# A macaron encoder block: three plain gate chunks at the start of the first feed-forward block, four block pairs instead of five, and another order at both openings

## The chip, the cores and the metric

The kernel runs on one core of one Trainium2 chip. The metric is device microseconds of one execution, as the median of several runs. The engines are called as in the profile: PE (TensorE, matrix products), DVE (VectorE), ACT (ScalarE), POOL (GpSimd) and SP (SyncE, which issues all loads).

## What is computed

One layer for 256 tokens of width 2048, all in float32. The change touches the two feed-forward blocks, the first and the last big stage:

```python
def _swiglu(x, wg, wu, wd):
    return (jax.nn.silu(x @ wg) * (x @ wu)) @ wd
h = h + 0.5 * _swiglu(_rmsnorm(h, ffn1_norm[i]), ffn1_wg[i], ffn1_wu[i], ffn1_wd[i])
a = _rmsnorm(h, mix_norm[i])
z = a @ w_in[i]                   # q, k, v of 8 heads; three parts of a gated short convolution
...
h = h + mixed @ w_out[i]
h = h + 0.5 * _swiglu(_rmsnorm(h, ffn2_norm[i]), ffn2_wg[i], ffn2_wu[i], ffn2_wd[i])
...                               # a gated per-layer embedding
return _rmsnorm(h, final_norm)
```

`wg` and `wu` are 2048 x 5632, `wd` is 5632 x 2048. The 5632 hidden columns are eleven chunks of 512.

## The kernel before

**Precision and tiles.** Each float32 operand is split into a high part (ACT, a copy to the PE's rounded format) and a low part (DVE, the difference). A product is three matmuls (`mm3`, lines 114 to 116): high x high, high x low, low x high. Weights come in tiles of 128 x 1024 (512 KB): SP loads `raw`, ACT writes `whi`, DVE writes `wlo`. There are 6 buffers each of `raw`, `whi` and `wlo`, so a tile can be prepared at most 6 tiles ahead of the one that PE works on.

**Items.** `unit_items` makes a unit of one chunk: 8 items for a gate or up chunk (`g0`, `u0`, `u1`, ...), 2 items for a column of `d0` (the down product of chunk 0), 4 for later down columns. An item has a preparation (load and split a tile) and a run (12 matmuls of 512 columns: 4 triples). `drive` lines the items up: it emits preparations until 6 tiles are held and then the run of the oldest item, so on ACT and DVE the work of an item stands behind the preparation of items up to 6 tiles later. After each run `pump()` emits one entry of `queue`, the side work: transposes of a finished chunk, factors, SiLU of a pair. Then, if it was the unit's last item, `done` emits the unit's eviction. The order so written holds on each engine.

**Banks.** A unit writes two PSUM tiles. With `wide` false they are always those with the tag `mm`, of which there are two: the next unit's first matmul waits until the unit before is evicted. With `wide` true the units go to `pa` and `mm` by turns.

**Pairs.** The gate product is done for chunk 0 by itself and for chunks 1 to 10 as five pairs by Winograd's form of Strassen's scheme: 7 half-size products in place of 8. A pair (`Pair`, names `ffn1s0` to `ffn1s4`) is 12 items: 8 of two tiles and 4 triples each, then 4 of three tiles and 6 triples, 56 triples in all where two plain gate chunks are 64; DVE has additions on the raw tiles besides. It uses combinations of the four quarters of the activations: `factors` makes them, one half chunk (c, p) a call, by four small DVE subtractions (`ffn1sv`), an ACT copy (`ffn1sh`) and a DVE difference (`ffn1sl`). `at` and `base` are the places in the stream of plain items ahead of which a pair's items stand. At a pair's end `whole` combines (6 DVE operations), then `queue` gets SiLU (ACT, 4 operations), `after` (products with the up chunk, lines 486 and 490) and `turn` (transposes).

**The norm.** The scale 1/rms is applied at the evictions. In the first block `load_x` loads `h` during `u0` and sums its squares on ACT; at the end of `u0`, `silu0` makes the scale (DVE, then POOL), applies SiLU to `g0` (`ffn1sg`) and `gated` (line 448) multiplies it with `u0`; then the transposes `ffn1gT` stand behind the next item's run. In the second block the scale is made by a queue entry.

**The opening of a block** is `g0`, `u0`, `u1`, `u2`, `d0` with pair 0 between their items.

Of the kernel before, what the change touches and what calls it, by code (L numbers as in the profile page):

```python
# [944 lines left out]
```

## Time and profile before

| what | value |
|---|---|
| median of 3 runs | 1963.72 us (1963.34 to 1965.5) |
| the profiled execution | 1965.0 us |
| its span, first to last instruction | 1962.9 us |
| mean granted TensorE clock | 0.989 of full speed |
| PE busy | 1910.3 us, 97% of the span |
| DVE busy, ACT busy | 1473.9 us, 1056.6 us |
| bytes read from HBM | 433.41 MB, 222 GB/s over the span |

The profiled execution is one of its own; 2.1 us of its time lie outside its span. A busy PE counts the modelled end of each matmul, so neighbouring matmuls overlap in the rows: the pace is read from start to start. "Idle before" a row is the time in which the engine did nothing, with what released it.

### The profile page before, as it was taken

The numbers are of one execution on the slowest core, as the hardware profiler recorded it, in microseconds if no ns is written. First come the engines' busy times: TensorE is split into PE (matmuls) and PEld (weight loads), VectorE is DVE, ScalarE is ACT, GpSimd is POOL, SyncE is SP. The second block draws the span as 40 slices with busy tenths as digits, with TensorE's granted clock in tenths as the row PEclk, the third lists the DMA queues.
The fourth block names the chain that finished last, engine by engine and source line by source line (L and its number), as shares of the span: only waits on it lengthen the run. The fifth ranks groups of instructions, "written<-read, shape, count | busy, mean of one in ns | idle before, by whom it ended". The sixth has DMA issues, their size and how long they took to land.

```text
span 1962.9 us, 23890 instructions
## 1 busy us (share of the span) xinstructions
PE 1910.3 (97%) x8649; PEld 1578.6 (80%) x8649; DVE 1473.9 (75%) x1712; ACT 1056.6 (54%) x1345; POOL 35.7 (2%) x36
## 2 busy tenths in 40 slices
PE   8898999999999999999999989989999999999998
PEld 6686888888888888888888868868888888888887
DVE  6877978879788765656656668778797887987664
ACT  7554555555555555555445555545555555555653
POOL 0000000000000000100000000000000000000010
PEclk9998999999999999999999999989999999999999
DMA  8575776777767765555555547747777667777652
GB/s 293 196 259 186 265 265 225 264 251 245 266 223 240 270 201 183 192 172 165 177 190 177 187 163 230 273 163 260 253 244 271 222 239 268 240 269 238 204 182 99
DMA packets 127206, 437.09 MB, mean 223 GB/s; under 512 B 13808, under 2 KB 14320, under 8 KB 126832
## 3 DMA queue, kind: packets, MB, share of 16 engines
q1 hardware_dynamic: 127088, 435.57, 65.7%
q8 instruction: 68, 1.11, 0.2%
q14 instruction: 50, 0.41, 0.1%
HBM read 433.41 MB, written 2.10 MB: 222 GB/s over the span
## 4 chain that ended last, share of the span: by engine, by line
PE 92%; DVE 3%; ACT 3%; issue 1%; DMA 1%; POOL 0%; ACTq 0%; SPq 0%; POOLq 0%; DVEq 0%
PE ffn2u L114 4%; PE ffn2u L116 4%; PE ffn2u L115 4%; PE ffn1d L114 4%; PE ffn2d L114 4%; PE ffn1d L116 4%; PE ffn1d L115 4%; PE ffn2d L116 4%; PE ffn2d L115 4%; PE ffn1u L114 4%; PE ffn1u L116 4%; PE ffn1u L115 4%; PE o L114 1%; PE o L116 1%; PE o L115 1%; PE pg L116 1%
## 5 line engine op out<-in xcount | busy, mean ns | idle before, releaser
L45 ACT ACTIVATE whi_ffn1s<-raw_ffn1s 128x1024 fp32r<-128x1024 f32 x120 | 126.2, 1061 | 169.6 <-DVE raw_ffn1s L347 38.0
L45 ACT ACTIVATE whi_ffn2s<-raw_ffn2s 128x1024 fp32r<-128x1024 f32 x120 | 126.0, 1061 | 165.3 <-DVE raw_ffn2s L347 39.7
L110 DVE TENSOR_TENSOR wlo_ffn2s<-raw_ffn2s,whi_ffn2s 128x1024 fp32r<-128x1024 f32 x120 | 144.6, 1221 | 14.0 <-ACT whi_ffn2s L45 9.7
L110 DVE TENSOR_TENSOR wlo_ffn1s<-raw_ffn1s,whi_ffn1s 128x1024 fp32r<-128x1024 f32 x120 | 144.7, 1221 | 11.1 <-ACT whi_ffn1s L45 6.5
L114 PE MATMUL ffn2u<-whi_ffn2u,aTh 128*128 128x512 f32 x352 | 138.5, 393 | 7.4 <-ACT ffn2sg L45 7.4
L114 PE MATMUL ffn1u<-whi_ffn1u,aTh 128*128 128x512 f32 x352 | 139.3, 396 | 5.7 <-DVE ffn1sg L448 3.4
L115 PE MATMUL ffn1u<-wlo_ffn1u,aTh 128*128 128x512 f32 x352 | 138.7, 394 | 4.0 <-DVE wlo_ffn1u L110 4.0
L110 DVE TENSOR_TENSOR wlo_ffn2u<-raw_ffn2u,whi_ffn2u 128x1024 fp32r<-128x1024 f32 x88 | 106.0, 1221 | 43.6 <-ACT whi_ffn2u L45 42.4
L116 PE MATMUL ffn1u<-whi_ffn1u,aTl 128*128 128x512 f32 x352 | 138.1, 392 | 0.0
L115 PE MATMUL ffn2u<-wlo_ffn2u,aTh 128*128 128x512 f32 x352 | 137.7, 391 | 0.0
L116 PE MATMUL ffn2u<-whi_ffn2u,aTl 128*128 128x512 f32 x352 | 137.7, 391 | 0.0
L110 DVE TENSOR_TENSOR wlo_ffn1u<-raw_ffn1u,whi_ffn1u 128x1024 fp32r<-128x1024 f32 x88 | 105.7, 1221 | 38.2 <-ACT whi_ffn1u L45 37.2
L45 ACT ACTIVATE whi_ffn2u<-raw_ffn2u 128x1024 fp32r<-128x1024 f32 x88 | 91.1, 1055 | 63.9 <-PE ffn2u L116 45.0
L110 DVE TENSOR_TENSOR wlo_ffn2d<-raw_ffn2d,whi_ffn2d 128x1024 fp32r<-128x1024 f32 x88 | 104.9, 1219 | 17.4 <-ACT whi_ffn2d L45 17.2
L45 ACT ACTIVATE whi_ffn1u<-raw_ffn1u 128x1024 fp32r<-128x1024 f32 x88 | 90.7, 1054 | 50.5 <-PE ffn1u L116 40.8
L110 DVE TENSOR_TENSOR wlo_ffn1d<-raw_ffn1d,whi_ffn1d 128x1024 fp32r<-128x1024 f32 x88 | 104.7, 1220 | 12.4 <-ACT whi_ffn1d L45 12.0
L45 ACT ACTIVATE whi_ffn2d<-raw_ffn2d 128x1024 fp32r<-128x1024 f32 x88 | 89.3, 1048 | 16.3 <-PE ffn2d L116 8.0
L45 ACT ACTIVATE whi_ffn1d<-raw_ffn1d 128x1024 fp32r<-128x1024 f32 x88 | 89.2, 1048 | 11.3 <-PE ffn1d L116 5.1
L114 PEld LDWEIGHTS ffn1u<-whi_ffn1u,aTh 128*128 128x128 f32 x352 | 66.6, 189 | 21.9 <-ACT whi_ffn1u L45 4.4
L114 PEld LDWEIGHTS ffn2u<-whi_ffn2u,aTh 128*128 128x128 f32 x352 | 66.6, 189 | 21.4 <-ACT ffn2sg L45 7.8
L115 PEld LDWEIGHTS ffn1u<-wlo_ffn1u,aTh 128*128 128x128 f32 x352 | 66.8, 190 | 19.6 <-DVE wlo_ffn1u L110 6.0
L116 PEld LDWEIGHTS ffn1u<-whi_ffn1u,aTl 128*128 128x128 f32 x352 | 66.7, 189 | 13.8
(809 smaller groups left out, 5108.9 us busy)
## 6 DMA issues: line engine op xcount, KB each, us to landing
raw_ffn1s<-in_ws SPq DMA_DIRECT2D x120, 512.0 KB, 5.5
raw_ffn2s<-in_ws SPq DMA_DIRECT2D x120, 512.0 KB, 5.4
raw_ffn1u<-in_wu SPq DMA_DIRECT2D x88, 512.0 KB, 5.1
raw_ffn1d<-in_wd SPq DMA_DIRECT2D x88, 512.0 KB, 4.9
raw_ffn2u<-in_wu SPq DMA_DIRECT2D x88, 512.0 KB, 5.1
raw_ffn2d<-in_wd SPq DMA_DIRECT2D x88, 512.0 KB, 4.8
raw_o<-in_wout SPq DMA_DIRECT2D x32, 512.0 KB, 4.5
raw_pg<-in_wpg SPq DMA_DIRECT2D x24, 512.0 KB, 4.6
```

The source lines that it names most:

```text
L45: nc.scalar.activation(out=out, in_=in_, func=func, **kw)
L110: tt(out=lo[:, sl], in0=raw[:, sl], in1=f(hi[:, sl]), op=ALU.subtract)
L114: nc.tensor.matmul(ps, lhsT=xh, rhs=wh, start=first, stop=False)
L115: nc.tensor.matmul(ps, lhsT=xh, rhs=wl, start=False, stop=False)
L116: nc.tensor.matmul(ps, lhsT=xl, rhs=wh, start=False, stop=last)
```

## The change

The first block no longer uses a pair for chunks 1 and 2: `first_opening` runs `g0`, `u0`, `g1`, `u1`, `d0`, `g2`, `u2` as plain units with `wide` true, and four pairs follow for chunks 3 to 10 (`quads(w, 1536)`). The calls of `factors` are spread: one for every second item of `u0` and `g1`, where before there was one for every item of `u0`. In `unit_items` the eviction of a finished unit is emitted ahead of the side work, where it stood behind it. In the second block the entry that makes the norm's scale stands ahead of the four factor entries, pair 0 stands at earlier places (`at` ends at 32, not 36), and the second product of `after` is a queue entry of its own. `WK` goes from 10 to 11 work buffers.

```diff
-    WK = 10
+    WK = 11
@@ unit_items, run
-            pump()
+            due = min(1, len(queue))
             if g == ng - 1 and s == 1:
                 done(st["ps"])
+            pump(due)
@@ Pair.whole
-            queue.extend([lambda: (silu(0), silu(1)), self.after, lambda: None, self.turn])
+            queue.extend([lambda: (silu(0), silu(1)), self.after]
+                         + [lambda: None] * self.gap + [self.turn])
@@ swiglu, pair
-            pr = Pair(nm, ws, i, gate)
+            pr = Pair(nm, ws, i - 1 if first else i, gate)
...
+            def after_b():
+                for t in range(2):
+                    tt(out=pr.c[2 * t + 1], in0=pr.ub[t], in1=pr.c[2 * t + 1], op=ALU.mult)
+                queue.append(turned([pr.c[1], pr.c[3]], 2, pr.sets))
...
                 if i == 0:
-                    for t in range(2):
-                        tt(out=pr.c[2 * t + 1], in0=pr.ub[t], in1=pr.c[2 * t + 1], op=ALU.mult)
-                    queue.append(turned([pr.c[1], pr.c[3]], 2, pr.sets))
+                    queue.append(after_b)
@@ swiglu
+        def both_plain(fc, g, sets, hooks):
+            if fc > 0:
+                def done(ps):
+                    for t in range(2):
+                        act(g[t], ps[t], AF.Silu, scale=gate["rstd"][:, t:t + 1])
+                yield from unit_items(wg, fc, f"{nm}g{fc}", aT, done, wide=True, late=hooks[0])
+
+            def done_up(pu):
+                if fc == 0:
+                    silu0()
+                gated(pu, g)
+                queue.append(turned(g, fc, sets))
+            yield from unit_items(wu, fc, f"{nm}u{fc}", aT, done_up, wide=True, late=hooks[1])
+
+        def first_opening(pr):
+            sets0 = []
+
+            def hook(o):
+                def late(g, s):
+                    if o == 0 and s == 0:
+                        load_x(g)
+                    if s == 0:
+                        factors(nm, o + g // 2, g % 2)
+                return late
+            yield from both_plain(0, g0, sets0, (None, hook(0)))
+            g1 = [wk(f"{nm}sg1_{t}") for t in range(2)]
+            yield from both_plain(1, g1, pr.sets, (hook(2), None))
+            yield from down(0, 1, sets0, False, True)
+            g2 = [wk(f"{nm}sg2_{t}") for t in range(2)]
+            yield from both_plain(2, g2, pr.sets, (None, None))
@@ swiglu, everything
                 yield from gate0(early)
-                at = [8, 10, 12, 14, 16, 18, 20, 21, 23, 24, 26, 28]
-                base = 32
+                at = []
+                base = 48
             else:
+                queue.append(lambda: gate.update(rstd=rstd_of(nm)))
                 for c in (2, 3):
                     for p in range(2):
                         queue.append(partial(factors, nm, c, p))
-                queue.append(lambda: gate.update(rstd=rstd_of(nm)))
-                at = [8, 11, 14, 16, 19, 22, 24, 26, 29, 32, 34, 36]
+                at = [8, 10, 13, 16, 18, 20, 22, 24, 26, 28, 30, 32]
                 base = 40
```

**Place A, the first block's first gated chunk.** On DVE, up to the gated product of `g0` (`ffn1sg0`), which the transposes wait for; before:

```order
L347 TENSOR_TENSOR raw_ffn1s0_0_0_524<-raw_ffn1s0_0_0_524,raw_ffn1s0_0_1_526 128x512
L348 TENSOR_TENSOR raw_ffn1s0_0_1_526<-raw_ffn1s0_0_0_524,raw_ffn1s0_0_1_526 128x512
L349 TENSOR_TENSOR raw_ffn1s0_0_1_526<-raw_ffn1s0_0_1_526,raw_ffn1s0_0_0_524 128x512
L110 TENSOR_TENSOR wlo_ffn1s0_0_0_532<-raw_ffn1s0_0_0_524,whi_ffn1s0_0_0_531 128x1024
L110 TENSOR_TENSOR wlo_ffn1s0_0_1_536<-raw_ffn1s0_0_1_526,whi_ffn1s0_0_1_535 128x1024
L110 TENSOR_TENSOR wlo_ffn1u1_0_0_554<-raw_ffn1u1_0_0_551,whi_ffn1u1_0_0_553 128x1024
L110 TENSOR_TENSOR wlo_ffn1u1_0_1_572<-raw_ffn1u1_0_1_569,whi_ffn1u1_0_1_571 128x1024
L225 TENSOR_REDUCE sm_ffn1_None_599<-ss_ffn1_0_339 128x1
L225 TENSOR_REDUCE sm_ffn1_None_599<-ss_ffn1_1_401 128x1
L228 TENSOR_SCALAR sm2_ffn1_None_602<-sm_ffn1_None_599 128x2
L448 SCALAR_TENSOR_TENSOR ffn1sg0_0_104<-ffn1u0_0_446,rstd_ffn1_None_604,ffn1sg0_0_104 128x512
L448 SCALAR_TENSOR_TENSOR ffn1sg0_1_105<-ffn1u0_1_447,rstd_ffn1_None_604,ffn1sg0_1_105 128x512
```

and in the changed kernel:

```order
L110 TENSOR_TENSOR wlo_ffn1g1_2_0_573<-raw_ffn1g1_2_0_570,whi_ffn1g1_2_0_572 128x1024
L318 TENSOR_TENSOR ffn1sv3_0_578<-a3_0_228 128x128
L319 TENSOR_TENSOR ffn1sv3_0_578<-a3_0_228 128x128
L320 TENSOR_TENSOR ffn1sv3_0_578<-a3_0_228,ffn1sv3_0_578 128x128
L321 TENSOR_TENSOR ffn1sv3_0_578<-a3_0_228,ffn1sv3_0_578 128x128
L323 TENSOR_TENSOR ffn1sl3_577<-ffn1sv3_0_578,ffn1sh3_576 128x4x128
L226 TENSOR_REDUCE sm_ffn1_None_597<-ss_ffn1_0_332 128x1
L226 TENSOR_REDUCE sm_ffn1_None_597<-ss_ffn1_1_385 128x1
L229 TENSOR_SCALAR sm2_ffn1_None_600<-sm_ffn1_None_597 128x2
L450 SCALAR_TENSOR_TENSOR ffn1sg0_0_104<-ffn1u0_0_423,rstd_ffn1_None_602,ffn1sg0_0_104 128x512
L450 SCALAR_TENSOR_TENSOR ffn1sg0_1_105<-ffn1u0_1_424,rstd_ffn1_None_602,ffn1sg0_1_105 128x512
L110 TENSOR_TENSOR wlo_ffn1g1_2_1_613<-raw_ffn1g1_2_1_610,whi_ffn1g1_2_1_612 128x1024
```

The two tiles of pair 0 and two of `u1` ahead of the norm have gone; five tiles of `g1` and three factor steps (of c = 2 and 3) stand ahead of it. On PE the transposes stood behind `u0`, one pair item and one item of `u1`; now they stand behind `u0` and one item of `g1`.

**Place C, the opening of the second block.** On ACT, from the last tile of `g0` (`ffn2g0_3_1`) to its SiLU (`ffn2sg0`); before:

```order
L45 ACTIVATE ffn2sh2_9291<-ffn2sv2_0_9293 128x4x128
L45 ACTIVATE ffn2sh2_9291<-ffn2sv2_1_9312 128x4x128
L45 ACTIVATE whi_ffn2s0_0_0_9326<-raw_ffn2s0_0_0_9319 128x1024
L45 ACTIVATE whi_ffn2s0_0_1_9330<-raw_ffn2s0_0_1_9321 128x1024
L45 ACTIVATE ffn2sh3_9346<-ffn2sv3_0_9348 128x4x128
L45 ACTIVATE whi_ffn2u0_0_0_9357<-raw_ffn2u0_0_0_9355 128x1024
L45 ACTIVATE ffn2sh3_9346<-ffn2sv3_1_9373 128x4x128
L45 ACTIVATE whi_ffn2u0_0_1_9382<-raw_ffn2u0_0_1_9380 128x1024
L45 ACTIVATE whi_ffn2u0_1_0_9407<-raw_ffn2u0_1_0_9405 128x1024
L45 ACT_TABLE_LOAD
L45 ACTIVATE ffn2sg0_0_9179<-ffn2g0_0_9217,rstd_ffn2_None_9403 128x512
```

and in the changed kernel:

```order
L45 ACTIVATE ffn2sh2_9207<-ffn2sv2_0_9209 128x4x128
L45 ACTIVATE whi_ffn2s0_0_0_9223<-raw_ffn2s0_0_0_9216 128x1024
L45 ACTIVATE whi_ffn2s0_0_1_9227<-raw_ffn2s0_0_1_9218 128x1024
L45 ACTIVATE ffn2sh2_9207<-ffn2sv2_1_9243 128x4x128
L45 ACTIVATE whi_ffn2u0_0_0_9252<-raw_ffn2u0_0_0_9250 128x1024
L45 ACTIVATE ffn2sh3_9268<-ffn2sv3_0_9270 128x4x128
L45 ACTIVATE whi_ffn2u0_0_1_9279<-raw_ffn2u0_0_1_9277 128x1024
L45 ACTIVATE ffn2sh3_9268<-ffn2sv3_1_9295 128x4x128
L45 ACT_TABLE_LOAD
L45 ACTIVATE ffn2sg0_0_9076<-ffn2g0_0_9114,rstd_ffn2_None_9193 128x512
```

The factor copies (`ffn2sh`) stand apart from one another, the third tile of `u0` has gone behind the SiLU, and the last factor copy still stands ahead of it.

**Place D, the end of the second block's pair 0.** On DVE, from the last tile of the `d0` columns 0 to 3 (`ffn2d0_3_0_1`) to the eviction of column 2 into `h`; before:

```order
L110 TENSOR_TENSOR wlo_ffn2d0_3_0_1_10348<-raw_ffn2d0_3_0_1_10345,whi_ffn2d0_3_0_1_10347 128x1024
L347 TENSOR_TENSOR raw_ffn2s1_0_0_10351<-raw_ffn2s1_0_0_10351,raw_ffn2s1_0_1_10353 128x512
L348 TENSOR_TENSOR raw_ffn2s1_0_1_10353<-raw_ffn2s1_0_0_10351,raw_ffn2s1_0_1_10353 128x512
L349 TENSOR_TENSOR raw_ffn2s1_0_1_10353<-raw_ffn2s1_0_1_10353,raw_ffn2s1_0_0_10351 128x512
L110 TENSOR_TENSOR wlo_ffn2s1_0_0_10359<-raw_ffn2s1_0_0_10351,whi_ffn2s1_0_0_10358 128x1024
L110 TENSOR_TENSOR wlo_ffn2s1_0_1_10363<-raw_ffn2s1_0_1_10353,whi_ffn2s1_0_1_10362 128x1024
L110 TENSOR_TENSOR wlo_ffn2d1_0_0_0_10387<-raw_ffn2d1_0_0_0_10384,whi_ffn2d1_0_0_0_10386 128x1024
L486 TENSOR_TENSOR ffn2s0c0_9982<-ffn2ua1_0_9895,ffn2s0c0_9982 128x512
L486 TENSOR_TENSOR ffn2s0c2_9984<-ffn2ua1_1_9896,ffn2s0c2_9984 128x512
L490 TENSOR_TENSOR ffn2s0c1_9983<-ffn2ub2_0_10153,ffn2s0c1_9983 128x512
L490 TENSOR_TENSOR ffn2s0c3_9985<-ffn2ub2_1_10154,ffn2s0c3_9985 128x512
L516 SCALAR_TENSOR_TENSOR h0_94<-ffn2d0_2_0_10366,h0_94 128x512
```

and in the changed kernel, from the first of the six operations of `whole` to the eviction of column 0:

```order
L406 TENSOR_TENSOR ffn2s0c0_9835<-ffn2s0c0_9835,ffn2s0x_10154 128x512
L407 TENSOR_TENSOR ffn2s0c2_9837<-ffn2s0c2_9837,ffn2s0x_10154 128x512
L408 TENSOR_TENSOR ffn2s0x_10154<-ffn2s0q5_9902,ffn2s0x_10154 128x512
L409 TENSOR_TENSOR ffn2s0c3_9838<-ffn2s0c3_9838,ffn2s0x_10154 128x512
L410 TENSOR_TENSOR ffn2s0c1_9836<-ffn2s0c1_9836,ffn2s0x_10154 128x512
L411 TENSOR_TENSOR ffn2s0c1_9836<-ffn2s0q3_9903,ffn2s0c1_9836 128x512
L110 TENSOR_TENSOR wlo_ffn2d0_1_0_1_10165<-raw_ffn2d0_1_0_1_10162,whi_ffn2d0_1_0_1_10164 128x1024
L110 TENSOR_TENSOR wlo_ffn2d0_2_0_0_10171<-raw_ffn2d0_2_0_0_10168,whi_ffn2d0_2_0_0_10170 128x1024
L110 TENSOR_TENSOR wlo_ffn2d0_2_0_1_10177<-raw_ffn2d0_2_0_1_10174,whi_ffn2d0_2_0_1_10176 128x1024
L110 TENSOR_TENSOR wlo_ffn2d0_3_0_0_10201<-raw_ffn2d0_3_0_0_10198,whi_ffn2d0_3_0_0_10200 128x1024
L522 SCALAR_TENSOR_TENSOR h0_94<-ffn2d0_0_0_10180,h0_94 128x512
L522 SCALAR_TENSOR_TENSOR h1_95<-ffn2d0_0_1_10181,h1_95 128x512
```

The pair ends ahead of column 0 where it ended ahead of column 2, and the evictions of columns 0 and 1 now stand behind the pair's combination and the tiles of later columns. On PE, at the seam of columns 0 and 1, before (a pair item's first product lies between):

```order
L115 MATMUL ffn2d0_0_1_10202<-wlo_ffn2d0_0_0_1_10138,ffn2g0h_9658 128x512
L116 MATMUL ffn2d0_0_1_10202<-whi_ffn2d0_0_0_1_10137,ffn2g0l_9659 128x512
L114 MATMUL ffn2s0q1_10064<-whi_ffn2s0_10_0_10183,aTh2_98 128x512
L115 MATMUL ffn2s0q1_10064<-wlo_ffn2s0_10_0_10184,aTh2_98 128x512
L116 MATMUL ffn2s0q1_10064<-whi_ffn2s0_10_0_10183,aTl2_102 128x512
```

and in the changed kernel:

```order
L115 MATMUL ffn2d0_0_1_10181<-wlo_ffn2d0_0_0_1_10111,ffn2g0h_9549 128x512
L116 MATMUL ffn2d0_0_1_10181<-whi_ffn2d0_0_0_1_10110,ffn2g0l_9550 128x512
L114 MATMUL ffn2d0_1_0_10228<-whi_ffn2d0_1_0_0_10132,ffn2g0h_9549 128x512
L115 MATMUL ffn2d0_1_0_10228<-wlo_ffn2d0_1_0_0_10133,ffn2g0h_9549 128x512
L116 MATMUL ffn2d0_1_0_10228<-whi_ffn2d0_1_0_0_10132,ffn2g0l_9550 128x512
```

The pair items that lay between columns 0, 1 and 2 have moved ahead of column 0. The seams of columns 0 to 3 now have no pair item between them.

## Rows read from the trace of the kernel before

**Rows 1.** Page: the span, and the busy time of TensorE with its share.
```profile
span 1962.9 us, 23890 instructions
...
PE 1910.3 (97%) x8649; PEld 1578.6 (80%) x8649; DVE 1473.9 (75%) x1712; ACT 1056.6 (54%) x1345; POOL 35.7 (2%) x36
```

**Rows 2.** Waits of PE: line, releaser; total us, times, longest.
```profile
PE ffn1d L114 <- DVE h L516: 9.6, 1, 9.6
PE ffn2d L114 <- DVE h L516: 9.6, 1, 9.6
PE ffn2u L114 <- ACT ffn2sg L45: 7.4, 1, 7.4
```

**Rows 3.** Timeline of PE, first block: start, us, instruction, [idle before].
```profile
31.24 0.39 PE L114 MATMUL ffn1u<-whi_ffn1u,aTh 128*128 128x512 f32 x1
...
72.78 0.79 PE L114 MATMUL ffn1u<-whi_ffn1u,aTh 128*128 128x512 f32 x1 [3.43 <-DVE ffn1sg L448]
...
77.09 1.04 PE L292 MATMUL ffn1gT<-ident,ffn1sg 128*128 128x128 f32 x8
```

**Rows 4.** Timeline of DVE, the first block's first 75 us.
```profile
28.11 1.23 DVE L110 TENSOR_TENSOR wlo_ffn1u<-raw_ffn1u,whi_ffn1u 128x1024 fp32r<-128x1024 f32 x1 [0.18 <-ACT whi_ffn1u L45]
29.26 0.29 DVE L317 TENSOR_TENSOR ffn1sv<-a 128x128 f32<-128x128 f32 x1
...
32.04 1.23 DVE L110 TENSOR_TENSOR wlo_ffn1u<-raw_ffn1u,whi_ffn1u 128x1024 fp32r<-128x1024 f32 x1 [0.26 <-ACT whi_ffn1u L45]
...
50.71 1.38 DVE L317 TENSOR_TENSOR ffn1sv<-a 128x128 f32<-128x128 f32 x1
...
59.60 1.23 DVE L110 TENSOR_TENSOR wlo_ffn1u<-raw_ffn1u,whi_ffn1u 128x1024 fp32r<-128x1024 f32 x1 [0.26 <-ACT whi_ffn1u L45]
...
69.91 0.21 DVE L225 TENSOR_REDUCE sm_ffn_None<-ss_ffn 128x1 f32<-128x4 f32 x2
...
71.98 1.41 DVE L448 SCALAR_TENSOR_TENSOR ffn1sg<-ffn1u,rstd_ffn_None,ffn1sg 128x512 f32<-128x512 f32 x2 [1.65 <-ACT ffn1sg L45]
```

**Rows 5.** Timeline of POOL, first block.
```profile
50.55 2.67 POOL L661 TENSOR_TENSOR bm<-bm,msk 128x512 f32<-128x512 f32 x2 [49.21 <-DMA bm<-in_bias]
```

**Rows 6.** Timeline of PE around the first block's longest wait.
```profile
165.02 0.39 PE L114 MATMUL ffn1d<-whi_ffn1d,ffn1g0h 128*128 128x512 f32 x1
...
169.78 0.39 PE L114 MATMUL ffn1d<-whi_ffn1d,ffn1g0h 128*128 128x512 f32 x1
...
180.18 0.76 PE L114 MATMUL ffn1d<-whi_ffn1d,ffn1g0h 128*128 128x512 f32 x1 [9.56 <-DVE h L516]
...
188.08 1.03 PE L292 MATMUL ffn1gT<-ident,ffn1s0c 128*128 128x128 f32 x8
```

**Rows 7.** Windows after that wait: busy by engine, granted clock, DMA share, GB/s.
```profile
180.00:184.00 4.00, 3.82 (x9) 3.07 (x10) 1.77 (x3) 0.00 (x0) 0.00 (x0) 0.50 0.31 82
```

**Rows 8.** Timeline of ACT, opening of the second block.
```profile
1154.67 0.63 ACT L45 ACTIVATE ffn2sh<-ffn2sv 128x512 fp32r<-128x512 f32 x1 [2.35 <-DVE ffn2sv L320]
...
1157.21 1.28 ACT L45 ACT_TABLE_LOAD   x1
1159.56 1.27 ACT L45 ACTIVATE ffn2sg<-ffn2g,rstd_ffn_None 128x512 f32<-128x512 f32 x2 [1.07 <-POOL rstd_ffn_None L231]
```

**Rows 9.** Timeline of PE, opening of the second block.
```profile
1160.30 0.79 PE L114 MATMUL ffn2u<-whi_ffn2u,aTh 128*128 128x512 f32 x1 [7.37 <-ACT ffn2sg L45]
```

**Rows 10.** Timeline of DVE, end of the second block's first pair.
```profile
1273.74 0.69 DVE L405 TENSOR_TENSOR ffn2s0c<-ffn2s0c,ffn2s0x 128x512 f32<-128x512 f32 x1 [0.30 <-ACT ffn2s0x L45]
...
1289.28 1.28 DVE L516 SCALAR_TENSOR_TENSOR h<-ffn2d,h 128x512 f32<-128x512 f32 x2
```

**Rows 11.** Timeline of PE, the same place.
```profile
1274.95 0.39 PE L114 MATMUL ffn2d<-whi_ffn2d,ffn2g0h 128*128 128x512 f32 x1
...
1290.11 0.76 PE L114 MATMUL ffn2d<-whi_ffn2d,ffn2g0h 128*128 128x512 f32 x1 [9.55 <-DVE h L516]
...
1297.69 1.03 PE L292 MATMUL ffn2gT<-ident,ffn2s0c 128*128 128x128 f32 x8
```

More of the change, by code (lines that the diff above doesn't have):

```diff
@@ L457, in up0, with up_a @@
             return unit_items(wu, 0, f"{nm}u0", aT, done, late=late)
-        def up_a(fc, pr, sets):
+        def up_a(fc, pr, sets, late=None):
             def done(pu):
@@ L464, in done @@
                 pr.ua = ua
-            return unit_items(wu, fc, f"{nm}u{fc}", aT, done)
+            return unit_items(wu, fc, f"{nm}u{fc}", aT, done, late=late)
         def up_b(fc, pr, sets):
@@ L480, in pair @@
         def pair(i):
-            pr = Pair(nm, ws, i, gate)
+            pr = Pair(nm, ws, i - 1 if first else i, gate)
             pr.sets = []
+            pr.gap = 0 if first and i == 0 else 1
+            def after_b():
+                for t in range(2):
+                    tt(out=pr.c[2 * t + 1], in0=pr.ub[t], in1=pr.c[2 * t + 1], op=ALU.mult)
+                queue.append(turned([pr.c[1], pr.c[3]], 2, pr.sets))
             def after():
@@ L527, in late, with later @@
                         load_x(g)
-                    factors(nm, g, s)
+                        factors(nm, g // 2, g % 2)
+                def later(g, s):
+                    if s == 0:
+                        factors(nm, 2 + g // 2, g % 2)
                 yield from up0(sets, late)
+                yield from up_a(1, pr, pr.sets, later)
+                yield from up_b(2, pr, pr.sets)
             else:
@@ L532, in opening @@
                 yield from up0(sets)
-            yield from ups(0, pr)
+                yield from ups(0, pr)
             yield from down(0, 1, sets, False)
+        def both_plain(fc, g, sets, hooks):
[16 more added lines that the diff above has]
+                        load_x(g)
+                    if s == 0:
+                        factors(nm, o + g // 2, g % 2)
[6 more added lines that the diff above has]
+            yield from both_plain(2, g2, pr.sets, (None, None))
         def plain_stream(prs):
-            yield from opening(prs[0])
+            yield from (first_opening if first else opening)(prs[0])
             for i in range(5):
@@ L570, in everything @@
             n = 0
-            steps = chain.from_iterable(pr.items() for pr in prs)
+            steps = chain.from_iterable(pr.items() for pr in (prs[1:] if first else prs))
             for place in places:
@@ L886, in tiles, with quads @@
         ).reshape(n // 512, k // 512, P, 2048)
-    def quads(w):
-        w = np.asarray(w)[0][:, 512:]
+    def quads(w, o):
+        w = np.asarray(w)[0][:, o:]
+        m = w.shape[1] // 1024
         return np.ascontiguousarray(
-            w.reshape(8, 2, P, 5, 2, 512)[:, (0, 1, 0, 1), :, :, (1, 0, 0, 1)]
-            .reshape(2, 2, 8, P, 5, 512).transpose(4, 2, 0, 3, 1, 5)).reshape(5, 8, 2, P, 1024)
+            w.reshape(8, 2, P, m, 2, 512)[:, (0, 1, 0, 1), :, :, (1, 0, 0, 1)]
+            .reshape(2, 2, 8, P, m, 512).transpose(4, 2, 0, 3, 1, 5)).reshape(m, 8, 2, P, 1024)
     def kmajor(a):
@@ L931 @@
         "mask": msk,
-        "wg1": tiles(ffn1_wg[:, :, :512]), "ws1": quads(ffn1_wg), "wu1": tiles(ffn1_wu), "wd1": tiles(ffn1_wd),
+        "wg1": tiles(ffn1_wg[:, :, :1536]), "ws1": quads(ffn1_wg, 1536), "wu1": tiles(ffn1_wu), "wd1": tiles(ffn1_wd),
         "win": tiles(w_in), "wout": tiles(w_out),
-        "wg2": tiles(ffn2_wg[:, :, :512]), "ws2": quads(ffn2_wg), "wu2": tiles(ffn2_wu), "wd2": tiles(ffn2_wd),
+        "wg2": tiles(ffn2_wg[:, :, :512]), "ws2": quads(ffn2_wg, 512), "wu2": tiles(ffn2_wu), "wd2": tiles(ffn2_wd),
         "wpg": tiles(ple_w_gate), "wpp": pw,
```

## The prediction

> **What bounds the kernel now.** I read the page first: PE is busy for 1910.3 of 1962.9 us [rows 1], so only two things can move the time: PE's work, and the 50 us in which it waits or runs slowly. The list of PE's waits says where they are: one wait of 9.6 us in each feed-forward block, on the eviction of `h`, and one of 7.4 us in the second block on the SiLU of `g0` [rows 2]. Each came once, so the four later pairs of each block, which end in the same way, have none. PE's timeline then gives pace and loss. From 165.02 to 169.78 seven triples start 0.68 us apart [rows 6], so an item of 4 triples is 2.72 us. After the wait, 8 triples took from 180.18 to 188.08, 7.90 us in place of 5.44: 2.46 us more [rows 6], and the windows show why: the granted clock is 0.50 of full, the 1.2 GHz level, after PE stood idle [rows 7]. Each long wait thus costs itself and some 2 us behind it. The first block's first 77 us lose more than their waits show: from 31.24 to the transposes at 77.09 PE does 40 triples (8 items of `u0`, a pair item, an item of `u1`), which are 27.20 us, and needs 45.85 [rows 3]. That is 18.65 us lost.
>
> **The change, part by part.**
>
> *More PE work: +5.4 us.* Two plain gate chunks are 64 triples, a pair is 56; 8 x 0.68 us [rows 6] = 5.44. All other matmuls stay. It lies on the path. In exchange 24 raw tiles become 16 and the pair's additions go; neither DVE nor loads bound that stretch, so this gains nothing by itself.
>
> *Place B, the first block's `d0`: -12.0 us.* The wait of 9.56 us comes because column 3's banks are those of column 2, whose eviction stands on DVE behind the end of pair 0. In the changed kernel no pair is in that stretch, and the units change banks by turns, so an eviction has a whole unit (5.44 us) of cover. The wait and its slow stretch go: 9.56 + 2.46 [rows 6]. What takes over is the first of the four pairs, in the place in which the later pairs of before stand, row for row; those have no such wait [rows 2]. If the first pair met one, it could keep 2 us.
>
> *Place A, the first block's `u0`: -1.9 us only.* Before, each item of `u0` costs DVE and ACT a chain: tile, factor step, next tile, 28.11 to 32.04, 3.93 us against PE's 2.72 [rows 4]. From 28.11 to 59.60 seven such steps took 31.49, so 3.98 more than 7 x 3.93: the squares of `h` and the eviction of `g0` on ACT, and two DVE operations of 1.38 instead of 0.29 us while POOL prepares two attention masks for 2.67 us [rows 4, 5]. Now every second tile has a step; a tile without one adds 1.15 us (28.11 to 29.26, [rows 4]). Two items are 3.93 + 1.15 = 5.08 us of the chain against 5.44 of PE, so `u0` itself no longer makes PE wait. But the transposes of `g0` stand on PE behind the first item of `g1`, and their source stands on DVE behind five tiles of `g1` and the seventh factor step (place A of the change). PE comes there at 31.24 + 36 x 0.68 = 55.7. DVE starts the tile of the seventh step at 28.11 + 6 x 5.08 + 3.98 = 62.6 (the squares, the eviction and the masks stay and fall into the same chain), ends that step 3.93 later, and needs from the norm's first reduction to the end of the gated product 69.91 to 73.39, 3.48 us [rows 4]: 70.0. PE waits 14.3 us, then has a slow stretch as at B, 2.46: 16.7 in place of 18.65. Bounds: without the 3.98 the loss is 12.8 (gain 5.9); if a plain tile costs 0.2 us of handshake more, 13 times, nothing is gained (-0.5). I take the middle sum, since squares and masks stay in the stretch. Late next: nothing, since four tiles of `g1` are ready when PE goes on.
>
> *Place C, the second block's norm: -1.4 us.* PE waits for the SiLU of `g0` because `u0` needs its banks. The scale is now made first, but the SiLU still stands on ACT behind the last factor copy (place C). That copy came at 1154.67 [rows 8] with one tile of `u0` ahead of it; now two are, and the reductions: some 1154.67 + 1.15 + 0.2 = 1156.0. Behind the copy (0.54 to the next start) comes a table load of 1.28, which before ran while ACT waited for the scale anyway [rows 8], and now is on the path: SiLU at 1157.9, PE 0.74 later (1159.56 to 1160.30, [rows 8, 9]) at 1158.6 to 1159. So some 1.4 us of the 7.37 [rows 9] go. Bounds: ACT was idle for 1.07 us behind the load [rows 8], put down to POOL; if that was the load's own, 0.3 is left; with the load hidden, 2.7. By the Trainium skill (page "ScalarE: Activation LUTs", section "What ACT_TABLE_LOAD costs") a switch of tables has a drain of about 1.38 us besides the load's 1.28; by that, estimated, nothing would be gained here and the sum would be 1.4 us worse. The rows speak against all of it, since the SiLU began 1.07 us behind the load's end.
>
> *Place D, the second block's `d0`: -2.2 us.* Here the units keep `wide` false. Pair 0 ends ahead of column 0, so the three seams of columns 0 to 3 have no pair item to cover the eviction (place D). Let 0 be the time at which PE ends the pair. Before, `whole` began 1.21 us ahead of that (1273.74 against 1274.95, [rows 10, 11]); now ACT has two evictions of `u2` first, and I put it at -0.6. Six operations of 0.69 overlapping to 4.1: 3.5; four tiles at 1.15: 8.1; then column 0's eviction, and PE 0.83 us after its start (1289.28 to 1290.11, [rows 10, 11]): 8.9. PE had finished column 0 at 5.44, so it waits 3.4. The second seam is covered by the transposes of chunk 1 (1.0 us). Between the evictions of columns 1 and 2 DVE has 7 operations on half tiles (0.65 each) and 3 tiles, 8.0 us, behind column 1's eviction (1.5), against PE's 1.0 + 5.44: there the transposes of chunk 2 and then column 3 wait some 2.8 together. 6.3 us of waits, and two slow stretches as after the 3.43 us wait in the first block (72.78 to 77.09 for 2.72 us of work, 1.6, [rows 3]): 9.5. Before it was 9.55 + 7.58 - 5.44 = 11.7 [rows 11]. Bounds: +1 if the second seam waits too, -5 if the short waits leave the clock at 2.4 GHz and chunk 2 comes in time.
>
> *Evictions ahead of side work: 0.* From the second pair on, the rows of ACT, DVE and SP are the same, one for one, as before. Their cover is the bank that the eviction frees a few operations earlier at most; without it the seams of rivals 3 and 4 are what it costs. `WK` costs only space.
>
> *Sum:* 5.4 - 12.0 - 1.9 - 1.4 - 2.2 = -12.1 us. The profiled execution took 1965.0, 2.1 of it outside the span, so it would take 1952.9; it lies 1.3 above the median of the runs, 1963.72, on which the forecast is **1951.6 us**.
>
> **The rivals.**
>
> 1. *Only B pays.* A's chain is as long as before (more handshakes) and D's new seams eat what they gave: 5.4 - 12.0 - 1.4 = -8.0, 1955.7. For it: both estimates are differences of larger numbers. Against: the chain has 3.93 + 1.15 for two items.
> 2. *The openings run free.* If the transposes of `g0` find their source ready, A's 16.7 us go: -12.1 - 16.7 = -28.8, 1934.9. If the rest of C's wait goes instead (7.37 - 1.4 = 6.0), -18.1, 1945.6. For it: `u0` itself is below PE's pace, and the scale is made earlier. Against: the five tiles ahead of the gated product, and the copy ahead of the SiLU.
> 3. *The wait only moves.* The 12 us of B come back at the end of the first pair, now under chunk 3: -0.1, 1963.6. Against: the later pairs of before [rows 2].
> 4. *Slower.* Each of the three bare seams of D costs what the one did, 11.7 us: 35.1 in place of 9.5, so -12.1 + 25.6 = +13.5, 1977. For it: same line, same banks. Against: `whole` and `after` stand before one eviction each, not before all three. It decides when D loses more than 25.5 us.
>
> **How the numbers follow.** The forecast as summed, 1948 to 1955, has 0.55, rival 1 0.15, rival 2 0.15, rival 3 0.09, rival 4 0.06. The table page's drain (a variant inside the forecast, 1953.0) has 0.1 of these. The bounds of the parts add up to 1944 and 1960; 8 in 10 lie in 1944.5 to 1957.5, which holds the forecast, rival 1 and the near part of rival 2. About 0.2% (3.9 us) is what can be told from no change. Faster by more than that: 0.86 (forecast and rivals 1 and 2), within it 0.08, slower 0.06.
>
> **What would show it.** PE's waits in the new profile: in the first block one wait near 56 us on DVE's gated product, of 10 to 15 us, and none on `h`; no wait inside `u0`; in the second block 6 us on the SiLU, then two or three waits on `h` or on `ffn2gT`, of 2 to 4 us each. The matmul count is up by 24. I am wrong if the wait at the transposes of `g0` is under 5 us (A's chain misread), if `h` still holds up the first block (B), or if a seam of D takes 8 us or more.

## The result and the profile after

The changed kernel takes 1951.61 us (median of 3 runs, 1950.43 to 1951.72), the kernel before 1963.72: a ratio of 0.9934, with a 95% interval of 0.9912 to 0.9957. The profiled execution took 1951.72 us, its span 1949.4. The page and the list of PE's waits after, which answer to [rows 1, 2]:

```profile
PE 1910.5 (98%) x8673; PEld 1582.2 (81%) x8673; DVE 1434.6 (74%) x1660; ACT 1041.3 (53%) x1326; POOL 36.1 (2%) x36
```
```profile
PE ffn1gT L293 <- DVE ffn1sg L450: 12.2, 2, 12.1
PE ffn2u L114 <- ACT ffn2sg L45: 6.2, 1, 6.2
PE ffn2d L114 <- DVE h L522: 4.7, 3, 2.7
...
PE ffn2gT L293 <- DVE ffn2s0c L489: 1.5, 2, 1.3
```

The 24 more matmuls are there, the wait on `h` in the first block (`ffn1d`) is not, and the wait on the SiLU is 1.1 us shorter. New are the wait of `ffn1gT` for the gated product, one of `ffn2gT` and three small ones on `h` in the second block.

Two instructions mark where the time came from: the first matmul of the second block (`ffn2g`) and the first of the per-layer embedding (`pg`). The views of one tile give the first and the last start of its matmuls by line. Before:

```profile
L114 PE MATMUL ffn2g<-whi_ffn2g,aTh x32: 389/389/481, 1127.2 to 1149.4; 128*128 128x512 f32 x32
L114 PE MATMUL pg<-whi_pg,aTh x128: 278/389/481, 1856.2 to 1949.8; 128*128 128x512 f32 x112, 128*128 128x256 f32 x16
```

After:

```profile
L114 PE MATMUL ffn2g<-whi_ffn2g,aTh x32: 389/389/481, 1116.7 to 1138.8; 128*128 128x512 f32 x32
L114 PE MATMUL pg<-whi_pg,aTh x128: 277/389/481, 1842.5 to 1936.0; 128*128 128x512 f32 x112, 128*128 128x256 f32 x16
```

Up to the second block the changed kernel is 10.5 us ahead, and in the second block it gains 3.2 more (1856.2 - 1127.2 = 729.0 before, 725.8 after). The parts behind `pg` and in between are the same.

PE's timeline at place A, after:

```profile
55.08 0.39 PE L114 MATMUL ffn1g<-whi_ffn1g,aTh 128*128 128x512 f32 x1
...
67.98 0.48 PE L293 MATMUL ffn1gT<-ident,ffn1sg 128*128 128x128 f32 x1 [12.06 <-DVE ffn1sg L450]
68.64 1.75 PE L293 MATMUL ffn1gT<-ident,ffn1sg 128*128 128x128 f32 x7 [0.18 <-DVE ffn1sg L450]
70.04 0.78 PE L114 MATMUL ffn1g<-whi_ffn1g,aTh 128*128 128x512 f32 x1
...
73.46 0.39 PE L114 MATMUL ffn1g<-whi_ffn1g,aTh 128*128 128x512 f32 x1
```

PE runs through `u0` and one item of `g1` at full pace and then stands. From 31.27 (first triple of `u0`) to 67.98 it does 36 triples, 24.5 us, so 12.2 are lost; the eight transposes take 2.06 us in place of about 0.8, and the stretch to 73.46 another 1.4. The loss at A is 14.9 us, where it was 18.65. With 5.4 us of added work, what is left of the 10.5 for B is 12.2. DVE's timeline at the same place, after:

```profile
29.07 0.28 DVE L318 TENSOR_TENSOR ffn1sv<-a 128x128 f32<-128x128 f32 x1
...
58.59 4.15 DVE L110 TENSOR_TENSOR wlo_ffn1g<-raw_ffn1g,whi_ffn1g 128x1024 fp32r<-128x1024 f32 x2 [0.26 <-ACT whi_ffn1g L45]
62.67 0.28 DVE L318 TENSOR_TENSOR ffn1sv<-a 128x128 f32<-128x128 f32 x1
...
65.11 0.21 DVE L226 TENSOR_REDUCE sm_ffn_None<-ss_ffn 128x1 f32<-128x4 f32 x2
...
67.17 1.41 DVE L450 SCALAR_TENSOR_TENSOR ffn1sg<-ffn1u,rstd_ffn_None,ffn1sg 128x512 f32<-128x512 f32 x2 [1.65 <-ACT ffn1sg L45]
```

The first of the seven factor steps begins at 29.07 and the last at 62.67; the norm's reduction comes 2.44 us behind the start of the last. PE goes on at 67.98, behind the first of the two gated products (the row of both ends at 68.58).

Place C in ACT's timeline, after, with the last factor copy, the table load and the SiLU, one behind the other; PE restarts at 1148.63 after 6.24 us:

```profile
1145.95 0.63 ACT L45 ACTIVATE ffn2sh<-ffn2sv 128x512 fp32r<-128x512 f32 x1 [2.34 <-DVE ffn2sv L321]
1146.60 1.28 ACT L45 ACT_TABLE_LOAD   x1
1147.89 1.26 ACT L45 ACTIVATE ffn2sg<-ffn2g,rstd_ffn_None 128x512 f32<-128x512 f32 x2
```

Place D in PE's timeline, after:

```profile
1261.52 0.47 PE L114 MATMUL ffn2d<-whi_ffn2d,ffn2g0h 128*128 128x512 f32 x1 [2.75 <-DVE h L522]
...
1267.86 0.48 PE L114 MATMUL ffn2d<-whi_ffn2d,ffn2g0h 128*128 128x512 f32 x1
...
1274.82 0.30 PE L293 MATMUL ffn2gT<-ident,ffn2s0c 128*128 128x128 f32 x1 [1.27 <-DVE ffn2s0c L489]
...
1277.16 0.47 PE L114 MATMUL ffn2d<-whi_ffn2d,ffn2g0h 128*128 128x512 f32 x1 [0.85 <-DVE h L522]
...
1288.33 0.47 PE L114 MATMUL ffn2d<-whi_ffn2d,ffn2g1h 128*128 128x512 f32 x1 [1.13 <-DVE h L522]
```

The first seam waits 2.75 us, the second not at all, the third first for the products of chunk 2 and then for `h`. The third wait on `h`, 1.13 us, is at the first column of the next down product.

### The profile page after: what moved, and what is told of

It reads as the page before. It is cut to its first block, busy times and chain, and to the rows that moved or that the text cites. A ratio compares the mean times of both kernels' runs of the same rounds, so it can differ in the third digit from the quotient of the medians.

```text
span 1949.4 us, 23819 instructions
## 1 busy us (share of the span) xinstructions
PE 1910.5 (98%) x8673; PEld 1582.2 (81%) x8673; DVE 1434.6 (74%) x1660; ACT 1041.3 (53%) x1326; POOL 36.1 (2%) x36
## 5 line engine op out<-in xcount | busy, mean ns | idle before, releaser
L45 ACT ACTIVATE whi_ffn1s<-raw_ffn1s 128x1024 fp32r<-128x1024 f32 x96 | 101.0, 1061 | 150.0 <-DVE raw_ffn1s L348 23.6
L110 DVE TENSOR_TENSOR wlo_ffn1s<-raw_ffn1s,whi_ffn1s 128x1024 fp32r<-128x1024 f32 x96 | 115.8, 1220 | 8.4 <-ACT whi_ffn1s L45 4.4
L116 PEld LDWEIGHTS ffn2u<-whi_ffn2u,aTl 128*128 128x128 f32 x352 | 66.8, 190 | 14.1
L115 PEld LDWEIGHTS ffn2u<-wlo_ffn2u,aTh 128*128 128x128 f32 x352 | 66.8, 190 | 13.7
```

The lines of the kernel that those rows point to most:

```text
L45: nc.scalar.activation(out=out, in_=in_, func=func, **kw)
L110: tt(out=lo[:, sl], in0=raw[:, sl], in1=f(hi[:, sl]), op=ALU.subtract)
L115: nc.tensor.matmul(ps, lhsT=xh, rhs=wl, start=False, stop=False)
L116: nc.tensor.matmul(ps, lhsT=xl, rhs=wh, start=False, stop=last)
```

## The experiments

Each kernel was timed against the kernel before on the same chip; a ratio stands for that. In these sets the kernel before took 1964.24 to 1964.87 us against 1963.72 above, so a difference between medians of two sets is good to about 1 us; where less is at stake, the traces decide.

**1. The eviction's place alone**, in the kernel before:

```diff
-            pump()
+            due = min(1, len(queue))
             if g == ng - 1 and s == 1:
                 done(st["ps"])
+            pump(due)
```

> The kernel before with one edit: a finished unit's eviction is emitted ahead of the side work. The order moves only at column 2 of d0 in both blocks: there four DVE products of some 0.62 us go behind the eviction. Theory (the wait at B and D is the queue on DVE ahead of the eviction): each of the two waits of 9.6 us falls by 2.5 us, 1963.7 - 5.0 = 1958.7. Rival (the prediction's price for this edit, 0, or the transposes of chunk 2 now wait instead): 1963.7.

Measured: 1959.32 us, ratio 0.9972 (0.9962 to 0.9981), against 1964.87. PE's waits and the mark in the second block:

```profile
PE ffn2d L114 <- DVE h L517: 7.2, 1, 7.2
PE ffn1d L114 <- DVE h L517: 7.2, 1, 7.2
```
```profile
L114 PE MATMUL ffn2g<-whi_ffn2g,aTh x32: 389/389/481, 1124.6 to 1146.8; 128*128 128x512 f32 x32
L114 PE MATMUL pg<-whi_pg,aTh x128: 277/389/481, 1850.6 to 1944.1; 128*128 128x512 f32 x112, 128*128 128x256 f32 x16
```

Both waits fall from 9.6 to 7.2 us, by the four products that left the queue ahead of the eviction. On DVE the eviction of column 3 has moved too, ahead of the two differences of the next transposes, which I had not said; no wait of PE hangs on it. The orders of PE, ACT and POOL are the same. The edit that I priced at nothing is worth 5.5 us by itself, 3.0 of it in the second block (726.0 against 729.0).

**2. The second block's opening put back** (queue order, `at`, `after_b`), the eviction's place kept.

```diff
-                queue.append(lambda: gate.update(rstd=rstd_of(nm)))
                 for c in (2, 3):
                     for p in range(2):
                         queue.append(partial(factors, nm, c, p))
-                at = [8, 10, 13, 16, 18, 20, 22, 24, 26, 28, 30, 32]
+                queue.append(lambda: gate.update(rstd=rstd_of(nm)))
+                at = [8, 11, 14, 16, 19, 22, 24, 26, 29, 32, 34, 36]
...
-                    queue.append(after_b)
+                    after_b()
```

> The changed kernel with the second block's opening put back (order of queue entries, places of pair 0, second product inside the first). Theory from the traces (the first block gave 10.5 us: +5.4 for work, -12.2 at B, -3.8 at A): 3 us slower than the changed kernel, 1954.6. Rival (the prediction's sum, first block -8.5, second -3.6): 1955.2 by its sum. Rival (the second block's edits give nothing): 1951.6.

Measured: 1953.02 us, ratio 0.9940 (0.9926 to 0.9955), which cannot be told from the changed kernel's 0.9934 and is 1951.9 us on the scale of 1963.72. PE's waits and the marks:

```profile
PE ffn2u L114 <- ACT ffn2sg L45: 7.4, 1, 7.4
PE ffn2d L114 <- DVE h L522: 7.2, 1, 7.2
```
```profile
L114 PE MATMUL ffn2g<-whi_ffn2g,aTh x32: 387/389/481, 1117.1 to 1139.2; 128*128 128x512 f32 x32
L114 PE MATMUL pg<-whi_pg,aTh x128: 277/389/481, 1843.1 to 1936.7; 128*128 128x512 f32 x112, 128*128 128x256 f32 x16
```

From `ffn2g` to `pg` it takes 726.0 us, the changed kernel 725.8. So with the eviction's place the second block has 3.0 of its 3.2 us, and the rest of the reordering adds no more than 0.2. That reordering changes which waits PE has (one of 7.2 us becomes 2.75, 1.5 and two of about 1; 7.4 becomes 6.2). They are some 2 us less in all, but the time is the same, so as much is lost behind them; for the wait at C the next experiment shows how. The rival that these edits give nothing is nearest. Whether they would give something without the eviction's new place was not tried.

**3. The scale last again**, alone, `at` as changed:

```diff
-                queue.append(lambda: gate.update(rstd=rstd_of(nm)))
                 for c in (2, 3):
                     for p in range(2):
                         queue.append(partial(factors, nm, c, p))
+                queue.append(lambda: gate.update(rstd=rstd_of(nm)))
```

> The changed kernel with the scale's entry of the second block behind the factor entries again. Theory (the earlier scale is worth what the trace shows at C: 7.37 - 6.24 = 1.1 us): 1952.7, with PE's wait on the SiLU back at 7.4 us. Rival (the table load hides behind it as before, nothing lost): 1951.6.

Measured: 1952.17 us, ratio 0.9936 (0.9921 to 0.9951), which fits both. The trace speaks for the rival: PE's wait is 6.8 us and not 7.4, and from `ffn2g` (1116.3) to `pg` (1842.2) it takes 725.9 us, so even these 0.6 us are given back. ACT's timeline in this kernel:

```profile
1145.31 1.28 ACT L45 ACT_TABLE_LOAD   x1
1148.08 1.27 ACT L45 ACTIVATE ffn2sg<-ffn2g,rstd_ffn_None 128x512 f32<-128x512 f32 x2 [1.48 <-POOL rstd_ffn_None L232]
```

The load now runs while ACT waits for the scale, as I had read it in the kernel before. Here what a shorter wait saves is lost behind it. These are windows of the second 4 us after PE's restart (length, busy time of PE, PEld, DVE, ACT and POOL, granted clock, DMA share, GB/s), of the kernel before (7.37 us of wait), of this kernel (6.84) and of the changed kernel (6.24):

```profile
1164.30:1168.30 4.00, 4.00 (x18) 3.28 (x17) 2.23 (x2) 1.16 (x2) 0.00 (x0) 0.94 0.85 249
...
1152.82:1156.82 4.00, 4.00 (x16) 3.23 (x15) 3.51 (x4) 1.37 (x2) 0.00 (x0) 0.84 0.86 259
...
1152.63:1156.63 4.00, 4.00 (x15) 3.18 (x14) 3.47 (x4) 1.36 (x2) 0.00 (x0) 0.73 0.82 265
```

PE has 18, 16 and 15 matmuls in them.

**4. The transposes of `g0` later**, in the changed kernel:

```diff
                 gated(pu, g)
+                if fc == 0:
+                    queue.extend([lambda: None] * 6)
                 queue.append(turned(g, fc, sets))
```

> The changed kernel with the transposes of g0 six items later (six empty queue entries ahead of them). Theory (PE waits for a source it does not need yet; but five tiles of g1 stand ahead of the gated product and the sixth behind it): the wait of 12.1 us and its slow stretch of 2.7 go, and a wait of 3 to 4 us for the sixth tile of g1 comes near 67 us; 11 us faster than the changed kernel, 1940.6. Rival (PE runs through, all goes): 1936.8. Rival (DVE bounds the opening, so the wait only moves to the tiles of g1): 1951.6.

Measured: 1940.25 us, ratio 0.9876 (0.9859 to 0.9892), 11.4 us less than the changed kernel. PE's timeline:

```profile
68.96 0.50 PE L114 MATMUL ffn1g<-whi_ffn1g,aTh 128*128 128x512 f32 x1 [1.00 <-ACT whi_ffn1g L45]
...
70.22 0.50 PE L115 MATMUL ffn1g<-wlo_ffn1g,aTh 128*128 128x512 f32 x1 [0.76 <-DVE wlo_ffn1g L110]
...
75.61 1.03 PE L293 MATMUL ffn1gT<-ident,ffn1sg 128*128 128x128 f32 x8
```

The wait of 12.1 us was for a source that nothing needed yet. In its place PE waits 1.8 us for the sixth tile of `g1`, half of what was expected, with the granted clock at 1.00 (2.4 GHz). In this profile `u0` began 1.2 us later than in the changed kernel (32.44 against 31.27), which hides as much of the gain.

**5. The attention masks late**, in the changed kernel: POOL's mask needs a zero made from the scale of the next norm.

```diff
+    zero = small.tile([P, 2], F32, tag="zero", name="zero", bufs=1)
+    nc.vector.tensor_scalar_mul(zero, rstd, 0.0)
+    nc.gpsimd.tensor_tensor(out=msk, in0=msk0, in1=zero[:, 0:1].broadcast_to([P, 64]), op=ALU.add)
```

> The changed kernel with the two attention masks prepared on POOL after the first block instead of inside it (POOL's additions need a zero made from the next norm). Theory (while POOL adds, DVE's two tiles of g1 took 4.15 us in place of 2.36): the wait at the transposes of g0 is 1.8 us shorter, 1949.8. Rival (the delay lies in the squares on ACT, not in POOL): 1951.6. Rival (attention then waits for the masks): above 1951.6.

Measured: 1949.93 us, ratio 0.9924 (0.9909 to 0.9939). The interval alone could not tell it from the changed kernel; the rows do. PE's wait at the transposes is 10.42 us in place of 12.06, and DVE's row that answers to 4.15 us above:

```profile
58.72 2.36 DVE L110 TENSOR_TENSOR wlo_ffn1g<-raw_ffn1g,whi_ffn1g 128x1024 fp32r<-128x1024 f32 x2 [0.26 <-ACT whi_ffn1g L45]
```

**6. The SiLU early** in the second block, in the changed kernel:

```diff
                         queue.append(partial(factors, nm, c, p))
+                    if c == 2:
+                        queue.extend([lambda: None] * 2)
```

> The changed kernel with the two factor entries of c = 3 in the second block put behind the SiLU of g0 (two empty entries ahead of them). Theory (the SiLU has scale and banks ready and only stands behind two factor steps of 3.9 us on ACT): the SiLU begins some 1.3 us after the end of g0 (the table load), PE's wait of 6.2 us falls under 1 us and its slow stretch of 3.0 us goes; as the steps now stand among the next tiles, PE waits 1 to 2 us for the second pair item. 6.5 us faster than the changed kernel, 1945.1. Rival (a switch of tables costs 1.4 us more than its load): 1946.5 or more, with that time to be seen between load and SiLU. Rival (the steps bound the opening, the wait only moves): 1951.

Measured: 1944.62 us, ratio 0.9898 (0.9883 to 0.9913). PE's wait on the SiLU is 0.3 us, and from `ffn2g` (1116.7) to `pg` (1835.2) it takes 718.5 us in place of 725.8. No wait for the second pair item came. ACT's timeline:

```profile
1138.63 1.99 ACT L45 ACTIVATE whi_ffn2u<-raw_ffn2u 128x1024 fp32r<-128x1024 f32 x2
1140.64 1.28 ACT L45 ACT_TABLE_LOAD   x1
1141.94 1.27 ACT L45 ACTIVATE ffn2sg<-ffn2g,rstd_ffn_None 128x512 f32<-128x512 f32 x2
```

**7. Both kinds of banks for the second block's `d0`**, in the changed kernel:

```diff
-            yield from down(0, 1, sets, False)
+            yield from down(0, 1, sets, False, True)
```

> The changed kernel with the second block's d0 in both kinds of banks by turns (pair 0 has ended there, so pa is free). Theory: the three waits on h (4.7 us together) go, the wait of 1.5 us for the products of chunk 2 stays, with less of a slow stretch: 4.5 us faster than the changed kernel, 1947.1. Rival (the next pair needs pa and now waits for the last column's eviction instead): 1951.6.

Measured: 1945.38 us, ratio 0.9902 (0.9887 to 0.9917). The waits on `h` inside `d0` are gone; the 1.1 us at the first column of the next down product stayed, so not all three went. The gain is larger than expected all the same, as the slow stretch of D is gone too: the granted clock is 1.00 from 1253 to 1261 and from 1271 to 1283 us. In PE's profile 5.5 us of the gain lie between `ffn2g` (1116.0) and `pg` (1836.3); the other 0.7 lie ahead of it, where the two kernels are alike.

**8. One kind of bank for the first block's `d0`**, in the changed kernel:

```diff
-            yield from down(0, 1, sets0, False, True)
+            yield from down(0, 1, sets0, False, False)
```

> The changed kernel with d0 of the first block in one kind of bank only, as the second block has it; the rows of DVE stay the same. Theory (at B both things count: without a pair DVE evicts at once, but each bare seam still costs the eviction, some 0.3 us until it starts and 0.83 us from there to PE): 3 or 4 waits of 1.1 us on h, 3.8 us slower than the changed kernel, 1955.4; the wait of 9.6 us does not come back. Rival (the pair's work on DVE was all of it, banks do not matter): 1951.6. Rival (the banks were all of it): a wait of 7 us or more comes back, 1959 or more.

Measured: 1954.33 us, ratio 0.9947 (0.9930 to 0.9964). PE's timeline:

```profile
120.41 0.47 PE L114 MATMUL ffn1d<-whi_ffn1d,ffn1g0h 128*128 128x512 f32 x1 [0.90 <-DVE h L522]
126.48 0.47 PE L114 MATMUL ffn1d<-whi_ffn1d,ffn1g0h 128*128 128x512 f32 x1 [0.38 <-DVE h L522]
132.55 0.47 PE L114 MATMUL ffn1d<-whi_ffn1d,ffn1g0h 128*128 128x512 f32 x1 [0.38 <-DVE h L522]
```

A column takes 6.07 us in place of 5.44. The intervals of the two kernels overlap, but `ffn2g` begins at 1119.9 us where it began at 1116.7. The waits are shorter than the 1.1 us that I had said. The wait of 9.6 us does not come back: without a pair DVE is free at the seam. The banks are worth some 3 us of the 12.

**9. Edits 4 to 7 together.**

> The changed kernel with the transposes of g0 six items later, the masks late, the SiLU of the second block early and its d0 in both kinds of banks. Theory (the four places are apart, so the gains add: 11.4 + 1.7 + 6.5 + 4.5): 24 us faster than the changed kernel, 1927.5. Rival (masks and transposes share one wait, so the masks give nothing more, and one of the others fails): 1934.

Measured: 1924.86 us, ratio 0.9798 (0.9782 to 0.9815). The gains add: by the four medians they are 11.4, 1.7, 7.0 and 6.2 us, 26.3 in all, and here 26.8. How much of the masks' 1.7 is left once the transposes are late was not settled, since `u0` began 0.9 us earlier here than in 4 (31.50 against 32.44).

**10. A pair kept in the first block**, with the edits of 9 and the weights cut for five pairs:

```diff
-            yield from (first_opening if first else opening)(prs[0])
+            yield from opening(prs[0])
...
-                at = []
-                base = 48
+                at = [8, 10, 12, 14, 16, 17, 18, 19, 21, 22, 23, 24]
+                base = 32
```

> The four edits of the run before, but the first block keeps five pairs: pair 0 among u1 and u2 and ended ahead of d0, factor steps at every second item of u0 and u1, d0 in both kinds of banks, the transposes of g0 six items late. PE does 8 triples less, 5.4 us. Theory (from u0 to d0 DVE has some 110 us of tiles, factor steps and additions against 103 us of PE, so DVE bounds this stretch): the gain is eaten by 7 us of waits on tiles of the pair, 1926.5, no better than with three plain chunks (1924.9). Rival (loads and DVE keep up): 1919.5.

Measured: 1937.58 us, ratio 0.9862 (0.9847 to 0.9876), slower than with three plain chunks, and by more than I had said. PE's waits:

```profile
PE ffn1u L114 <- DVE ffn1sg L450: 6.3, 1, 6.3
PE ffn1u L114 <- ACT ffn1ua L45: 4.3, 1, 4.3
```

The rest of the first block's waits in that list are 1.4 us and shorter. My mechanism was wrong: PE does not wait for the pair's tiles, but for the evictions of `u0` and `u1`. The pair holds `pa` and `pb`, so `u1` and `u2` must have the banks of the unit before, whose eviction stands on DVE or ACT behind the pair's tiles. How much of it is the banks and how much the queue ahead of the evictions was not taken apart. This is one placing of the pair; others were not tried.

**11. The transposes of chunk 2 later** in the second block, with the edits of 9:

```diff
-                queue.append(turned([pr.c[1], pr.c[3]], 2, pr.sets))
+                queue.extend([lambda: None, turned([pr.c[1], pr.c[3]], 2, pr.sets)])
```

> The four edits together, and the transposes of chunk 2 in the second block one item later. Theory (PE waits 1.5 us there for products that it needs only some 18 us later): 1.5 us faster than with the four, 1923.4. Rival (the next chunk's column then waits for them, or the difference is under what can be told): 1924.9.

Measured: 1921.10 us, ratio 0.9778 (0.9763 to 0.9792), 3.8 us less than 9. The two longest waits on work that are left in PE's list:

```profile
PE ffn1g L114 <- ACT whi_ffn1g L45: 3.4, 2, 3.0
...
PE ffn1g L115 <- DVE wlo_ffn1g L110: 0.8, 1, 0.8
```

The 1.5 us for chunk 2 are gone, and with them the 1.1 us on `h` at the next down product, which stood behind those transposes. That is 2.6 us by the list, which counts only the time in which PE did nothing. From `ffn2g` (1103.6) to `pg` (1812.1) it takes 708.5 us, in run 9 711.9 (1103.8 to 1815.7), so 3.4 of the 3.8 us lie in the second block; the remaining 0.4 are less than runs of one kernel differ by (1924.59 to 1925.38). This kernel is the fastest, 2.2% below the kernel before.

## Why the prediction was right, and where not

The forecast, 1951.6 us, is the measured time to a few hundredths, and that is better than its sum. Against the profiled execution the sum said -12.1 us, and 1965.0 to 1951.72 is -13.3; the two profiles lie differently to their medians (1.3 above, 0.1 above), which took up the difference. That it fits so closely is luck. Step by step:

- **PE's work, +5.4.** 24 matmuls more, 8 triples, and no other change in pace. Right by the count; the work was not timed apart.
- **Place B, -12.0.** Measured -12.2 by the balance above, with no wait on `h` in the first block and none at the end of its first pair, so rival 3 is out. The experiments say what it is made of: the eviction's place takes 2.4 us off the wait (1), the banks are worth some 3 us (8), and without either change of banks the wait stays away because no pair's end stands on DVE ahead of the eviction (8). The parts overlap and were not made to add up.
- **Place A, -1.9.** Mis-sized: -3.8. The mechanism, place and cause were as said, a wait at 56 us on the gated product, 12.1 us where 14.3 was worked out. PE went on at 67.98 us and not at 70.0, as three terms were too large. The squares, the eviction and the masks were put at 3.98 us; from the first factor step to the seventh it took 33.60 us (29.07 to 62.67), 3.12 more than 6 x 5.08, so 0.9 less. "Ends that step 3.93 later" takes the distance from one tile to the next; the step's own tile (1.15) and the step up to the norm (2.44) are 3.59, so 0.3 less. And the transposes begin behind the first of the two gated products, 0.6 us ahead of the end of both. The rest, 0.2, is an earlier start of the chain. The masks stayed on the path as said (5).
- **Place C, -1.4.** The wait fell by 1.1 us, with the load on the path as worked out, but that bought next to nothing: with the scale last again the time is the same (3). The sum took the wait alone and left out that the slow stretch behind it could grow.
- **Place D, -2.2.** The second seam was free, the first waited 2.75 us where 3.4 was said, and the third 2.1 (1.27 and 0.85) where 2.8 was said. The 1.13 us at the next down product were not in the sum, and there was one slow stretch where two were charged. But experiment 2 shows that, with evictions first, the order of `at` and of `after_b` gains nothing here.
- **Evictions ahead of side work, 0.** This is the step that was wrong. I compared rows from the second pair on, where nothing moved, and gave the openings' gain to the places B and D. Alone the edit takes 5.5 us from the kernel before (1), 3.0 of them in the second block, where the whole change takes 3.2; the -3.6 that C and D had in my sum is about the right sum, and this edit is enough for nearly all of it.
- **The table's drain.** The Trainium skill (page "ScalarE: Activation LUTs", section "What ACT_TABLE_LOAD costs") has about 1.38 us of drain beside the load. In the changed kernel the SiLU begins 0.01 us after the load's end, in experiment 6 0.02 us, and there the load begins 0.02 us after the copy ahead of it: here the switch costs its 1.28 us and no more, and the measurement decides.
- **Rival 1** (only B pays) is out for A, which gave 3.8 us, but near the truth for D: the new order there gives no more than 0.2 us on top of the eviction's place.
- **Rival 4** (each bare seam of D costs 11.7 us) is out: the largest took 2.75. **Rival 2** (the openings run free) did not come by itself, but experiments 4 and 6 show that a few queue entries in each block bring most of it.
- **Two small sums** are off, without consequence: the lower bound at A is -0.7 by its own terms (1.9 less 13 x 0.2), not -0.5, and the forecast with rivals 1 and 2 has a chance of 0.85, not 0.86.

## What to carry to other kernels

A wait at a transpose or a side step is not a bound by itself: ask when its result is first needed, and if that is later, move the step and not its source; here that gave 11.4 us, nearly as much as the whole change. Price an edit that reorders side work by making or undoing it alone, since a sum by places can be right while its parts belong to other edits. What a block scheme saves in matmuls it can lose at its place: in the one placing tried, 8 triples less came with 12.7 us more, as plain units that shared one pair of banks waited for evictions behind the pair's tiles.
